# Mixers of a two-layer streaming trunk: four projected groups with the weights stationary and both token blocks moving, and one chain of small steps for both blocks

## The chip, the cores and the metric

The kernel runs on one core of a Trainium2 chip. The metric is device time in microseconds for one execution. Five engines work side by side, each on its own queue of instructions: TensorE (PE, matrix products and transposes into PSUM), VectorE (DVE), ScalarE (ACT), GpSimd (POOL) and SyncE (SP), which issues the DMAs here. Semaphores order them where one needs what another has made, or a buffer that another still reads.

## The reference

Two layers over 256 tokens of width 1024. Each layer is a half-step of a gated feed-forward network (1024 to 2 x 2816, back to 1024), then token mixers that read one combined input projection and are joined by one output projection, then a second feed-forward half-step. A residual with a factor and a layer norm close each of the three parts.

```python
for l in range(DEPTH):
    x = layer_norm(ALPHA * x + 0.5 * swiglu(x, ffn1_w_gu[l], ffn1_w_down[l]), ln1_g[l], ln1_b[l])
    h = x @ w_in[l]
    dq, dk, dv, mz, mxbc, mdt, gq, gk, gv, gz, gb, ga = jnp.split(h, IN_SPLITS, axis=-1)
    a_out = diff_attention_mixer(dq, dk, dv, ...)          # softmax maps, 4 heads
    m_out = mamba2_mixer(mz, mxbc, mdt, m_conv_w[l], ...)  # conv of 4 taps, silu, state-space, 8 heads
    g_out = gated_deltanet_mixer(gq, gk, gv, gz, gb, ga, g_conv_w[l], ...)  # conv, silu, triangular solve, 4 heads
    mix = jnp.concatenate([a_out, m_out, g_out], -1) @ w_out[l]
    x = layer_norm(ALPHA * x + mix, ln2_g[l], ln2_b[l])
    x = layer_norm(ALPHA * x + 0.5 * swiglu(x, ffn2_w_gu[l], ffn2_w_down[l]), ln3_g[l], ln3_b[l])
```

The depthwise convolution runs along the tokens, over mxbc (1024 channels) and over gq, gk and gv (768 channels). The solve in DeltaNet is against unit lower triangles of 64 x 64, one per head and chunk of 64 tokens.

## The kernel before

The 256 tokens are two blocks of 128. Weights come in units: by DMA into one of five raw buffers, then in two exact parts, the high part by a ScalarE cast (L230, wh) and the low part by a VectorE subtraction (L231, wl). A product is three: high by high, low by high, high by low (`mm3`, L219 to L226). The transposed tokens xh and xl are stationary, and 512 columns of weights move. Both blocks use a unit while it is there; block 1 follows block 0 by four units, five at the ends of a segment (`order`, L1019).

Each block has its own PSUM tiles: two of one bank for the large products (ps, po) and two for everything else (aux). The pools of small SBUF tiles are also per block.

A feed-forward group is a PSUM tile of 256 gate and 256 up columns. When it is complete, ScalarE takes the silu (sg, L395), VectorE multiplies (hh, L397), TensorE transposes hh twice (hTps) and the result is split into hT for the down projection.

In the mixers, the columns of w_in are projected in seven groups: qk (512 columns), v with the gates (272), dqk, m0, m1, mz and dvz (512 each). `job` spawns a chain of small steps behind each group and block. Groups that are convolved are copied out of PSUM by ScalarE token-major, transposed by TensorE (gqkps, gvps, mxps, mbcps: 56 transposes in the two layers), copied into xc with three columns of halo from the other block, and convolved: two taps on ScalarE, two on VectorE (L435 to L445), then silu. `after_qk` (L530) then makes squares (sq), their sums (ssps), a power on GpSimd (r), K·K and Q·K products (laps), and from these LA; ktok is a transpose of the keys. `inverse` (L671) solves the triangles in five doubling levels: products gps, G on VectorE (L698), products ups, a subtraction into TT (L715), a transpose T on VectorE (L693). `decays` (L465) makes the decay matrices: ar on GpSimd (L503), dps on TensorE, ex on ScalarE (L523). `after_dqk` does attention (scps, aps), `after_m0` and `after_m1` the state-space part (xsps, cbps, yps).

Chains are generators. A step yields a time, and its next step is emitted when that much TensorE work, times a factor from a table (`PACE`, one entry per step), has been emitted. The framework then orders instructions per engine and places the semaphores by tiles and buffers.

Of the kernel before, what the change touches and what calls it, by code (L numbers as in the profile page):

```python
# [27 lines left out]
TAPS = 2  # taps of the convolutions on ScalarE  # L28
SP = 2  # pieces in which a unit of weights is split
WS = 19  # tiles of half a bank for a block of tokens  # L30
# [5 lines left out]
PACE = {  # L36
    "after_v": (0.25, 1.49),
    "decays": (0.36, 0.48, 0.28, 1.01, 0.39, 0.56),
    "after_qk": (0.33, 0.24, 0.66, 0.33, 0.33, 0.33, 0.23, 0.33, 0.5, 0.2, 0.28, 0.33, 0.33, 0.28, 0.33),
    "after_m0": (0.33, 1.09, 0.78, 0.47, 0.78),  # L40
    "after_m1": (0.29, 0.19, 0.07, 0.14, 0.29, 0.24, 0.29),
    "after_mz": (0.39, 0.58, 0.58, 0.47, 0.58),
    "after_dqk": (0.41, 0.69, 0.27, 0.19, 0.27, 0.19, 0.54, 0.14, 0.41, 0.27),
    "after_dvz": (0.48, 0.71, 1.17, 0.39, 0.28, 1.12),
    "gdn_out": (0.12, 0.19, 0.23, 0.39),
    "norm": (0.28, 0.33),
    "after_gu": (4.67, 2.45, 2.33),
}
ORD = (1, 0, 4, 2, 3, 5, 6)
WORD = (4, 5, 2, 3, 6, 7, 0, 1)  # L50
# [3 lines left out]
# columns of the constants  # L54
# [6 lines left out]
# columns of w_in, in the order in which they are projected  # L61
WIN = (
    ("v", ((2824, 256), (3336, 8), (2304, 8))),
    ("qk", ((2312, 512),)),
    ("m0", ((1280, 512),)),
    ("m1", ((1792, 512),)),
    ("dqk", ((0, 512),)),
    ("mz", ((768, 512),)),
    ("dvz", ((512, 256), (3080, 256))),
# [7 lines left out]
def constants():  # L77
    """Masks, the identity and the rotary tables: they depend on shapes alone."""
# [21 lines left out]
class Kernel:  # L100
    def __init__(self, ctx, tc, a, out):
# [6 lines left out]
        self.w_p = [pool("wA", WS), pool("wB", WS)]  # L108
        self.h_p = [pool("hA", 5), pool("hB", 5)]
        self.s_p = [pool("sA", 20), pool("sB", 20)]  # L110
# [11 lines left out]
    def w(self, b, shape, name, dt=F32):  # L122
        assert int(np.prod(shape)) <= 528
        return self.w_p[b].tile([P, *shape], dt, tag="w", name=self.name(name))

    def h(self, b, shape, name, dt=F32):
        assert int(np.prod(shape)) <= 256
        return self.h_p[b].tile([P, *shape], dt, tag="h", name=self.name(name))

    def s(self, b, n, name):  # L130
        assert n <= 32
        t = self.s_p[b].tile([P, 32], F32, tag="s", name=self.name(name))
        return t[:, :n]

    def aux(self, b, name):
        return self.aux_p[b].tile([P, 512], F32, tag="aux", name=self.name(name))

# [1 line left out]
    def setup(self):  # L139
# [12 lines left out]
        self.neghalf = c.tile([P, 8], F32, name="neghalf")  # L152
# [7 lines left out]
    def setup_late(self):  # L160
        """What the mixers need, loaded and prepared behind the first products."""
# [53 lines left out]
    def mm3(self, ps, xh, xl, ws, start, stop):  # L215
        """ps[n] += x.T @ w[n] for the parts (xh, xl) and the list of (wh, wl)."""
# [50 lines left out]
    def ready(self, u, b):  # L267
        st = self.st[b]
        if u["kind"] in ("gu", "win"):
            return st["xseg"] == u["seg"] and len(st["xT"]) > u["part"] // 2  # L270
# [849 lines left out]
```

## Time and profile before

| | |
|---|---|
| runs (us) | 1134.03, 1136.46, 1136.87; median 1136.46 |
| profiled execution, span | 1134.7 us, its own time 1134.7 us from first to last instruction |
| TensorE busy | 1108.1 us, 5301 products and transposes |
| VectorE busy | 740.0 us, 1541 instructions |
| ScalarE busy | 590.4 us, 1250 instructions |
| DMA | 184.92 MB, mean 163 GB/s |
| mixers of layer 0 | about 202 to 345 us of the span |

A row of a group reads: line, engine, operation, output and inputs by name, shapes, count, then busy time and mean ns of one, then the idle time of the engine just before it and what ended that. A row of waits reads: engine and instruction, the releaser, then the sum in us, the times and the longest. A row of a window has start and end, its length, the busy time and count of PE, PEld, DVE, ACT and POOL, the granted TensorE clock as a part of full speed, the DMA share and GB/s. A row of the timeline has the start in us, the duration, and the instruction; x4 are four in a run. Durations of products overlap their neighbours, so the distance of starts tells what one takes.

### The profile page before, as it was taken

Reading aid. Unit: us, or ns where it says so; the run is one execution under the profiler, and the core shown is the slowest. Engines: PE = TensorE matmul, PEld = TensorE weight load, DVE = VectorE, ACT = ScalarE, POOL = GpSimd, SP = SyncE. Lnnn points to the kernel's source line nnn. Section 1 sums busy time; section 2 is a strip of 40 time slices with the busy share of each in tenths; the row PEclk is TensorE's granted clock in tenths of the full one; section 3 lists DMA queues with packets and bytes.
Section 4 is the critical chain, followed back from the end, with each engine's and each line's share of the span. In section 5 each row is a group of like instructions: output and inputs, shape, how many; then the busy total and the mean of one; then the engine's idle time right before and its main releaser. Section 6 shows DMA issues by size and latency. Waiting matters only on the chain.

```text
span 1134.7 us, 15487 instructions
## 1 busy us (share of the span) xinstructions
PE 1108.1 (98%) x5301; PEld 896.1 (79%) x5301; DVE 740.0 (65%) x1541; ACT 590.4 (52%) x1250; POOL 86.3 (8%) x123
## 2 busy tenths in 40 slices
PE   7999999999998999999999999999999999999996
PEld 6888888867887888888888888888688878888885
DVE  5565555896778955554575565477867887555545
ACT  5565444773674454554445454449546644555440
POOL 0000000032012100000000000001501120000001
PEclk9999999997999999999999999999989999999999
DMA  8775555631224565555575655555311347555650
GB/s 285 237 221 183 187 185 151 196 119 49 70 85 143 191 203 184 185 185 186 167 230 179 186 185 185 186 154 184 111 38 51 108 142 239 182 184 175 186 165 37
DMA packets 138374, 184.92 MB, mean 163 GB/s; under 512 B 15160, under 2 KB 111800, under 8 KB 138296
## 3 DMA queue, kind: packets, MB, share of 16 engines
q1 hardware_dynamic: 138296, 183.95, 52.2%
q8 instruction: 41, 0.67, 0.2%
q14 instruction: 37, 0.30, 0.1%
HBM read 182.86 MB, written 1.05 MB: 162 GB/s over the span
## 4 chain that ended last, share of the span: by engine, by line
PE 91%; DVE 5%; POOL 2%; ACT 1%; issue 1%; DMA 0%; SPq 0%; POOLq 0%; DVEq 0%; ACTq 0%
PE ps L219 18%; PE ps L220 18%; PE ps L226 16%; PE po L220 8%; PE po L219 8%; PE po L226 7%; PE ups L326 2%; PE ps L222 2%; PE gps L326 2%; PE hTps L235 2%; DVE wl L231 1%; PE scps L326 1%; PE xps L235 1%; POOL rsq L367 1%; PE yps L326 1%
## 5 line engine op out<-in xcount | busy, mean ns | idle before, releaser
L231 DVE TENSOR_TENSOR wl<-raw,wh 128x512 fp32r<-128x512 f32 (+1 forms) x672 | 437.5, 688 | 255.3 <-ACT wh L230 250.5
L230 ACT CAST wh<-raw 128x512 fp32r<-128x512 f32 (+1 forms) x672 | 380.8, 614 | 329.1 <-PE ps L226 186.6
L219 PE MATMUL ps<-wh,xh 128*128 128x512 f32 x928 | 374.8, 405 | 2.9 <-ACT wh L230 2.7
L220 PE MATMUL ps<-wl,xh 128*128 128x512 f32 x928 | 368.5, 397 | 0.0
L226 PE MATMUL ps<-wh,xl 128*128 128x512 f32 (+1 forms) x812 | 322.3, 398 | 0.0
L219 PEld LDWEIGHTS ps<-wh,xh 128*128 128x128 f32 x928 | 176.5, 190 | 39.4 <-ACT wh L230 3.3
L220 PEld LDWEIGHTS ps<-wl,xh 128*128 128x128 f32 x928 | 176.6, 190 | 37.3 <-DVE wl L231 1.8
L226 PEld LDWEIGHTS ps<-wh,xl 128*128 128x128 f32 x812 | 154.6, 190 | 35.0 <-issue 1.3
L219 PE MATMUL po<-wh,hT 128*128 128x512 f32 x352 | 139.1, 395 | 0.0
L220 PE MATMUL po<-wl,hT 128*128 128x512 f32 x352 | 138.2, 393 | 0.0
L226 PE MATMUL po<-wh,hT 128*128 128x512 f32 x336 | 105.6, 394 | 0.0
L220 PEld LDWEIGHTS po<-wl,hT 128*128 128x128 f32 x352 | 66.2, 188 | 14.7
L219 PEld LDWEIGHTS po<-wh,hT 128*128 128x128 f32 x352 | 66.1, 188 | 14.7
L226 PEld LDWEIGHTS po<-wh,hT 128*128 128x128 f32 x336 | 63.1, 188 | 14.0
L365 POOL TENSOR_SCALAR rs<-mv 128x1 f32<-128x1 f32 x12 | 6.5, 538 | 793.9 <-DVE mv L349 793.9
L397 DVE TENSOR_TENSOR hh<-ps,sg 128x256 f32<-128x256 f32 x88 | 37.0, 420 | 43.0 <-ACT sg L395 43.0
L395 ACT ACTIVATE sg<-ps 128x256 f32<-128x256 f32 x88 | 33.9, 385 | 55.0 <-PE ps L222 54.7
L222 PE MATMUL ps<-wh,xl 128*128 128x512 f32 (+1 forms) x116 | 46.0, 397 | 0.0
L230 ACT CAST hT<-hTps 128x256 fp32r<-128x256 f32 x88 | 32.5, 369 | 17.0 <-PE hTps L235 17.0
L231 DVE TENSOR_TENSOR hT<-hTps,hT 128x256 fp32r<-128x256 f32 x88 | 35.1, 420 | 0.1
L235 PE MATMUL hTps<-cst,hh 128*128 128x128 f32 x176 | 34.0, 272 | 0.0
L235 PEld LDWEIGHTS hTps<-cst,hh 128*128 128x128 f32 x176 | 24.6, 140 | 11.8
(247 smaller groups left out, 1008.3 us busy)
## 6 DMA issues: line engine op xcount, KB each, us to landing
raw<-in_ffn_w_gu_dram SPq DMA_DIRECT2D x352, 256.0 KB, 3.2
raw<-in_ffn_w_down_dram SPq DMA_DIRECT2D x88, 512.0 KB, 3.5
raw<-in_w_in_dram SPq DMA_DIRECT2D x40, 512.0 KB, 4.5
raw<-in_w_out_dram SPq DMA_DIRECT2D x16, 512.0 KB, 3.6
raw<-in_w_in_dram SPq DMA_DIRECT2D x24, 256.0 KB, 2.8
g<-in_ln_g_dram SPq DMA_DIRECT2D x6, 512.0 KB, 5.0
b<-in_ln_b_dram SPq DMA_DIRECT2D x6, 512.0 KB, 4.9
x<-in_x_dram SPq DMA_DIRECT2D x4, 256.0 KB, 5.8
```

Of the source, the lines that this page charges most:

```text
L219: mm(p, lhsT=xh, rhs=wh, start=start, stop=False)
L220: mm(p, lhsT=xh, rhs=wl, start=False, stop=False)
L222: mm(p, lhsT=xl, rhs=wh, start=False, stop=True)
L226: mm(p, lhsT=xl, rhs=wh, start=False, stop=False)
L230: self.nc.scalar.copy(hi, src)
L231: self.nc.vector.tensor_tensor(lo, src, hi.bitcast(F32), op=ALU.subtract)
L235: self.nc.tensor.transpose(ps[:, n * P : (n + 1) * P], t, self.ident)
L326: self.nc.tensor.matmul(out, lhsT=lhsT, rhs=rhs, start=start, stop=stop)
L365: nc.gpsimd.tensor_scalar(t, ap, mul, add, op0=ALU.mult, op1=ALU.add)
L367: nc.gpsimd.tensor_tensor(r, t, self.neghalf[:, :n], op=ALU.pow)
L395: nc.scalar.activation(sg, ps[:, 0:256], AF.Silu)
L397: nc.vector.tensor_mul(hh, ps[:, 256:512], sg)
```

## The change

Four groups of the input projection (qk, m0, v, m1) are projected the other way round: a 128 x 128 tile of weights is stationary and the transposed tokens of both blocks move, 256 columns at a time. PSUM then holds channels on partitions and the tokens of both blocks side by side, and the convolution reads it there. The token-major copies, the 56 transposes and the halo copies are gone. The other groups are dqk, gd (272: the attention's values and the gates), mz and gz, still per block. The order of groups is dqk, gd, qk, m0, v, m1, mz, gz.

The chains of decays, qk with the inverse, v, m0 and m1 run once, with both blocks' tokens (eight heads in the inverse). Attention stays per block. ar moves from GpSimd to VectorE. Products of laps, scps and rps that use different row groups of the array are emitted alternately.

PSUM is two tiles ps of two banks (both blocks, or both halves of an output) and four aux tiles of one bank. The SBUF pools are shared by the blocks. The table of paces is empty, so each step uses 0.39; a transpose counts 0.107 us rather than 0.213 in the emission clock, and `after_gu` yields 3. In feed-forward the blocks follow each other by one unit between the ends, five at the ends. Each product of the feed-forward is as before.

```diff
-NEAR = 4
-PACE = {
...
-}
-ORD = (1, 0, 4, 2, 3, 5, 6)
-WORD = (4, 5, 2, 3, 6, 7, 0, 1)
+PACE = {}
+WORD = (0, 1, 6, 7, 2, 3, 4, 5)
...
 WIN = (
+    ("dqk", ((0, 512),), None),
+    ("gd", ((512, 256), (3336, 8), (2304, 8)), None),
+    ("qk", ((2312, 512),), (256, 0, 384, 128)),
+    ("m0", ((1280, 512),), (0, 128, 256, 384)),
+    ("v", ((2824, 256),), (0, 128)),
+    ("m1", ((1792, 512),), (0, 128, 256, 384)),
+    ("mz", ((768, 512),), None),
+    ("gz", ((3080, 256),), None),
 )
...
-        self.ps_p = [pool("psA", 2, **psum), pool("psB", 2, **psum)]
-        self.aux_p = [pool("auxA", 2, **psum), pool("auxB", 2, **psum)]
+        self.ps_p = pool("ps", 2, **psum)
+        self.aux_p = pool("aux", 4, **psum)
...
+    def ps(self, name):
+        return self.ps_p.tile([P, 1024], F32, tag="ps", name=self.name("ps"))
...
+            if u["both"]:
+                for i, c0 in enumerate(u["tiles"]):
+                    o = g["ps"][:, 256 * i : 256 * i + 256]
+                    for kk in range(ks):
+                        k = u["part"] * ks + kk
+                        xh, xl = (t[:, :, k % 4, :] for t in self.xT[k // 4])
+                        s = slice(kk * width + c0, kk * width + c0 + P)
+                        end = last and kk == ks - 1
+                        for n, (a, x) in enumerate(((wh[:, s], xh), (wh[:, s], xl), (wl[:, s], xh))):
+                            self.nc.tensor.matmul(
+                                o, lhsT=a, rhs=x, start=k == 0 and n == 0 and i % 2 == 0, stop=end and n == 2,
+                                skip_group_check=True,
+                            )
...
-        ps = self.aux(b, name + "ps")
-        self.transposes([src[:, k * P : (k + 1) * P] for k in range(n)], ps)
-        xc = self.w(b, [n, P + 3], name + "xc")
-        nc.scalar.copy(xc[:, :, 3:], ps[:, : n * P].rearrange("p (k t) -> p k t", k=n))
...
+        x = ps[:, : 256 * n].rearrange("p (i t) -> p i t", i=n)
+        before = self.big([n, 256], name + "tap")
+        for j in range(0, n, 2):
+            pair = list(enumerate(tiles))[j : j + 2]
+            for i, t in pair:
...
+                    nc.scalar.activation(acc[:, i], x[:, i], AF.Copy, scale=col(3, t))
+                nc.scalar.activation(before[:, i, 1:], x[:, i, 0:255], AF.Copy, scale=col(2, t))
+            a = acc[:, j : j + 2, 1:]
+            nc.vector.tensor_add(a, a, before[:, j : j + 2, 1:])
+            for i, t in pair:
+                for k in (1, 0):
+                    d = 3 - k
+                    nc.vector.scalar_tensor_tensor(
+                        acc[:, i, d:], in0=x[:, i, 0 : 256 - d], scalar=col(k, t), in1=acc[:, i, d:],
+                        op0=ALU.mult, op1=ALU.add,
+                    )
...
+        for n in range(3):
+            ex = self.big([2, 4, P], "ex")
+            for b in range(2):
+                r = self.w([4, P], "ar")
+                ve.tensor_tensor(
...
-            for hd in range(4):
-                self.mm(pg[:, 64 * hd : 64 * hd + 64], lhsT=LT(hd), rhs=col1(T[:, hd, :], 0))
+            for e in range(8):
+                self.mm(pg[:, 64 * e : 64 * e + 64], lhsT=LT(e), rhs=col1(T[:, e, :], 0))
...
+        opening = lambda at, hi: max(1, LAG - at[1] // 2)
+        closing = lambda at, hi: min(LAG, max(1, LAG - (hi - at[0]) // 2))
+        phase(0, first, opening)
+        out.extend((None, i) for i in range(first, stop))
+        phase(stop, n, closing)
```

How this moves the instructions is seen at three places. Names carry a number for each tile.

The first is TensorE where m0's group (ps_2525) ends and v's (ps_2816) begins in layer 0. In the change the steps of qk follow seven products later:

```order
L288 MATMUL ps_2525<-xl_1871,wh_2324 128x256
L288 MATMUL ps_2525<-xh_1870,wl_2325 128x256
L288 MATMUL ps_2816<-xh_1847,wh_2415 128x256
L288 MATMUL ps_2816<-xl_1848,wh_2415 128x256
L288 MATMUL ps_2816<-xh_1847,wl_2416 128x256
...
L342 MATMUL ssps_2568<-cst,sq_2515 128x2 x8
L342 MATMUL laps_2589<-qk_2493 128x256
L342 MATMUL laps_2590<-qk_2493 128x256
```

On ScalarE, the convolution of qk (reading ps_2262, the tile that ps_2816 takes over) stands there among the exponentials of the decays (ex from dps) and weight casts:

```order
L558 ACTIVATE ex_2432<-dps_2441 128x512
L472 ACTIVATE qk_2493<-ps_2262,cw 128x256
L473 ACTIVATE gqktap_2494<-ps_2262,cw 128x255
L558 ACTIVATE ex_2432<-dps_2452 128x512
L472 ACTIVATE qk_2493<-ps_2262,cw 128x256
L473 ACTIVATE gqktap_2494<-ps_2262,cw 128x255
L226 CAST wh_2798<-raw_2467 128x512 x2
L472 ACTIVATE qk_2493<-ps_2262,cw 128x256
L473 ACTIVATE gqktap_2494<-ps_2262,cw 128x255
```

In the kernel before, no step of a convolution read ps; the tile was free after one copy.

The second place is the inverse on TensorE. Before, products of the groups (ps) and the other block's inverse stood between its levels:

```order
L326 MATMUL gps_2588<-T_2367,LA_2350 128x64
L326 MATMUL gps_2588<-T_2367,LA_2356 128x64
L219 MATMUL ps_2768<-wh_2307,xh_1987 128x512
L220 MATMUL ps_2768<-wl_2308,xh_1987 128x512
L226 MATMUL ps_2768<-wh_2307,xl_1988 128x512
L219 MATMUL ps_2768<-wh_2307,xh_1987 128x512
L326 MATMUL ups_2638<-TT_2366,G_2553 128x64 x4
```

Now eight heads go together, and the first three levels stand in a row behind v's last product, ahead of m1's group (ps_2972):

```order
L288 MATMUL ps_2816<-xh_1870,wl_2462 128x256
L342 MATMUL gps_2663<-T_2630,LA_2588 128x64 x4
L342 MATMUL gps_2663<-T_2630,LA_2605 128x64 x4
L342 MATMUL ups_2679<-TT_2629,G_2634 128x64 x8
L342 MATMUL gps_2706<-T_2630,LA_2588 128x64 x4
L342 MATMUL gps_2706<-T_2630,LA_2605 128x64 x4
L342 MATMUL ups_2722<-TT_2629,G_2689 128x64 x8
L342 MATMUL gps_2741<-T_2630,LA_2588 128x64 x4
L342 MATMUL gps_2741<-T_2630,LA_2605 128x64 x4
L288 MATMUL ps_2972<-xh_1847,wh_2517 128x256
```

VectorE has m0's convolution (xsT from ps_2525) between the steps of these levels:

```order
L751 TENSOR_TENSOR G_2634<-gps_2663,cst 128x256x2
L475 TENSOR_TENSOR xsT_2776<-xsT_2776,mxtap_2777 128x2x255
L479 SCALAR_TENSOR_TENSOR xsT_2776<-ps_2525,cw,xsT_2776 128x254
L768 TENSOR_TENSOR TT_2629<-TT_2629,ups_2679 128x256x2
L479 SCALAR_TENSOR_TENSOR xsT_2776<-ps_2525,cw,xsT_2776 128x253
L746 STREAM_TRANSPOSE T_2630<-TT_2629 128x1024
L479 SCALAR_TENSOR_TENSOR xsT_2776<-ps_2525,cw,xsT_2776 128x254
L479 SCALAR_TENSOR_TENSOR xsT_2776<-ps_2525,cw,xsT_2776 128x253
L751 TENSOR_TENSOR G_2689<-gps_2706,cst 128x128x4
```

The third place is the end of a feed-forward group on TensorE. Block 0's last product is L218 here; five products of the next group (ps_1010) follow, and then block 1's last six in the same tile ps_906:

```order
L218 MATMUL ps_906<-wh_820,xl_156 128x512
L215 MATMUL ps_1010<-wh_841,xh_130 128x512
L216 MATMUL ps_1010<-wl_842,xh_130 128x512
L222 MATMUL ps_1010<-wh_841,xl_131 128x512
L215 MATMUL ps_1010<-wh_841,xh_130 128x512
L216 MATMUL ps_1010<-wl_842,xh_130 128x512
L215 MATMUL ps_906<-wh_820,xh_155 128x512
```

Before, block 1 had a tile of its own, some twenty products behind.

More of the change, by code (lines that the diff above doesn't have):

```diff
@@ L267, in ready @@
     def ready(self, u, b):
-        st = self.st[b]
         if u["kind"] in ("gu", "win"):
-            return st["xseg"] == u["seg"] and len(st["xT"]) > u["part"] // 2
-        return u["k"] // 2 in st["hT" if u["kind"] == "down" else "mT"]
+            n = u["part"] * u["ks"] // 4
+            return all((u["seg"], n, i) in self.xready for i in ((0, 1) if u["both"] else (b,)))
+        return (u["k"] // 2, b) in (self.hT if u["kind"] == "down" else self.mT)
     def job(self, u, b):
-        st = self.st[b]
@@ new lines, in job @@
+            last = u["part"] == KD // ks - 1
+            if u["both"]:
[11 more added lines that the diff above has]
+                            )
+                        self.clock += 3 * 256 / 2400
+                    if i < len(u["tiles"]) - 1:
+                        self.step()
+                if last:
+                    self.spawn(u["then"](u, g["ps"]))
+                return
@@ L647, in after_qk @@
[L647 to L659 removed]
+            LA.append(t)
@@ new lines, in after_qk @@
+            yield 0.5
+        b4 = lambda t: t.unsqueeze(2).to_broadcast([P, 4, 64])
+        x4 = self.h(0, [4, 64], "x4")
+        de = self.s(0, 4, "de")
+        ve.tensor_mul(de, d[:, 0:4], erev[:, 0, 0:4])
+        pk = self.aux(0, "ktok")
+        self.transposes([qk[:, 0, 0:P], qk[:, 2, 0:P]], pk)
+        ve.tensor_tensor(x4, pk[:, 0:256].rearrange("p (h d) -> p h d", h=4), b4(de), op=ALU.mult)
+        TT = yield from self.inverse(LA)
+        yield from self.until("gv")
+        rhs = self.w([8, 64], "rhs")
@@ L728, in inverse @@
-        yield 0.9
-        return TT
-    def after_m0(self, l, b, ps):
-        nc, st = self.nc, self.st[b]
-        hm = self.w(b, [512], "hm")
-        nc.scalar.copy(hm, ps)
-        yield 0.8
-        xsT = self.conv(l, b, hm, (0, 1, 2, 3), "m", "mx")
-        yield 6
-        yield from self.until(b, "E")
-        pt = self.aux(b, "xsps")
-        self.transposes([xsT[:, k] for k in range(4)], pt)
+            ve.tensor_tensor(cols(TT, 1), cols(TT, 1), view(pu), op=ALU.subtract)
+        yield 1.5
@@ L792, in after_m1, with after_mz @@
-        if b == 1:
-            yield 0.2
-            pf = self.aux(b, "yfps")
+        ve.tensor_add(y[:, 1], y[:, 1], t)
+        self.mx["y"] = y
+    def after_mz(self, l, b, ps):
+        nc = self.nc
+        ve = nc.vector
+        if b == 0:
+            self.sz = self.big([2, 512], "sz")
+        sz = self.sz
+        nc.scalar.activation(sz[:, b], ps, AF.Silu)
+        if b == 0:
+            return
+        yield 0.3
+        yield from self.until("y")
+        y = self.mx["y"].rearrange("p b h d -> p b (h d)")
+        ss = self.s(b, 4, "mss")
+        for i in range(2):
+            ve.tensor_mul(y[:, i], y[:, i], sz[:, i])
@@ L808, in after_m1 @@
[L808 to L824 removed]
+                q = self.h(b, [256], "msq")
@@ L996, in mix @@
             units = []
-            for name, cols in (WIN[i] for i in ORD):
-                for part in range(4):
+            for name, cols, tiles in WIN:
+                group = {}
+                width = sum(n for _, n in cols)
+                ks = 4 if width == 256 else 2
+                for part in range(KD // ks):
                     units.append(
-                        dict(kind="win", l=l, w=a["w_in"][l], name=name, part=part, cols=cols,
-                             width=sum(n for _, n in cols), then=self.after_win)
+                        dict(kind="win", l=l, w=a["w_in"][l], name=name, part=part, cols=cols, width=width, ks=ks,
+                             group=group, both=tiles is not None, tiles=tiles, then=self.after_win)
                     )
```

904 lines of the change are left out of this document (437 added, 467 removed).

## The prediction

> **What bounds the kernel now.** I read the page first, then the waits of TensorE, then the clock.
>
> ```profile
> span 1134.7 us, 15487 instructions
> PE 1108.1 (98%) x5301; PEld 896.1 (79%) x5301; DVE 740.0 (65%) x1541; ACT 590.4 (52%) x1250; POOL 86.3 (8%) x123
> PE xps L235 <- DMA x<-in_x_dram: 4.2, 1, 4.2
> PE ktok L235 <- DVE LA L576: 4.0, 2, 2.0
> PE mTps L235 <- DVE y L827: 3.2, 4, 1.1
> PE ps L219 <- ACT wh L230: 2.7, 1, 2.7
> PE dops L326 <- DVE mT L231: 2.1, 2, 1.1
> PE dps L326 <- POOL ar L503: 0.6, 2, 0.3
> PE mTps L235 <- DVE do L954: 0.5, 2, 0.3
> PE laps L326 <- DVE ss L550: 0.4, 2, 0.2
> 345.00:800.00 455.00, 452.78 (x2081) 367.11 (x2081) 292.63 (x557) 232.57 (x478) 20.34 (x29) 1.00 0.59 183
> ```
>
> TensorE is busy 1108.1 of 1134.7 us. Its waits sum to 17.7 us: 6.9 at the start (xps, wh), the other 10.8 in the mixers, 5.4 a layer, none longer than 2.0. In the long stretch of feed-forward (the row 345 to 800; its columns run PE, PEld, DVE, ACT, POOL, then clock) TensorE is busy 452.8 of 455 us at full clock. So nothing is to be won there, and the mixers hold what can be won or lost besides TensorE's own work. The third thing is the clock:
>
> ```profile
> 250.00:300.00 50.00, 50.00 (x269) 39.90 (x268) 34.94 (x91) 24.23 (x61) 11.89 (x15) 0.86 0.22 64
> 260.00:262.00 2.00, 2.00 (x17) 1.88 (x17) 0.88 (x4) 0.36 (x1) 1.16 (x1) 1.00 0.82 249
> 264.00:268.00 4.00, 4.00 (x13) 2.95 (x13) 2.83 (x11) 0.00 (x0) 0.36 (x1) 0.50 0.00 0
> 800.00:820.00 20.00, 17.79 (x88) 13.02 (x86) 15.94 (x42) 9.07 (x21) 9.12 (x8) 0.91 0.42 119
> 820.00:834.00 14.00, 14.00 (x54) 10.58 (x53) 8.48 (x26) 3.45 (x14) 3.04 (x5) 0.63 0.07 19
> ```
>
> The granted clock falls to 0.50 once in each layer's mixers. It costs 50 x 0.14 = 7.0 us in layer 0 and 20 x 0.09 + 14 x 0.37 = 7.0 us in layer 1. From 260 to 262 TensorE was busy all the time, though only with small float32 products, and the clock fell right after.
>
> **TensorE's work, -3 us a layer.** Prices are distances from start to start, since products overlap:
>
> ```profile
> 202.02 0.40 PE L220 MATMUL ps<-wl,xh 128*128 128x512 f32 x1
> 205.27 0.39 PE L219 MATMUL ps<-wh,xh 128*128 128x512 f32 x1
> 207.34 0.29 PE L219 MATMUL ps<-wh,xh 128*128 128x272 f32 x1
> 207.98 0.29 PE L226 MATMUL ps<-wh,xl 128*128 128x272 f32 x1
> 208.10 0.68 PE L235 MATMUL gqkps<-cst,hq 128*128 128x128 f32 x4
> 208.54 0.37 PE L219 MATMUL ps<-wh,xh 128*128 128x272 f32 x1
> 208.75 0.29 PE L220 MATMUL ps<-wl,xh 128*128 128x272 f32 x1
> ```
>
> Fourteen products of 512 columns lie between 202.02 and 205.27: 0.232 us each. Five of 272 columns take 207.34 to 207.98: 0.128. The line through both gives an estimate of 0.121 for 256 columns, which the trace has not in this form. Four transposes take 208.10 to 208.54, 0.11 each, and the product behind them comes 0.21 rather than 0.128 later, 0.08 for the way back. A layer gives up 192 products of 512 columns (44.5 us) for 384 of 256 (46.5): +2.0. The 28 transposes of the token-major projections go: -3.1, and some 14 returns from them: -1.1. The cumulative sums and C·B products change shape, about -0.5. Sum: -2.7, say -3. The copies out of PSUM, halo copies and half of the short DVE steps that vanish were beside TensorE and give nothing by themselves.
>
> The laps, scps and rps products now alternate between row groups of the array. Side by side they could take half: laps 1.05 us for four and scps 0.64 for four here,
>
> ```profile
> 243.58 1.13 PE L326 MATMUL laps<-gqkacc 64*128 64x256 f32 x4 [0.19 <-DVE ss L550]
> 255.02 0.71 PE L326 MATMUL scps<-dkT,dqT 32*128 32x128 f32 x4
> 308.30 0.45 PE L326 MATMUL sps<-vnew,x 128*64 128x64 f32 x8
> ```
>
> that is 4.2 us a layer for sixteen laps, 2.6 for sixteen narrow scps and 4.2 for sixteen wide ones, at the price of a laps. The halves give at most -5.5. That such pairs can overlap is shown by sps, which alternate between column halves: the row behind those eight starts at 308.68, 0.048 each. What follows is VectorE work on each result, though, so most of it would turn into waiting. I take -1, bounds 0 and -5.5.
>
> By the Trainium skill, TensorEngine Tiling (Array Packing), Key Properties, different tiles of the array load and multiply in parallel; by that alone the sum would be about 9 us lower for both layers. The sps row agrees for column halves, and no row of before has row groups alternating.
>
> **The waits of the mixers, +15 us a layer.** Four groups now leave one PSUM tile for both blocks, and there are two such tiles. The convolution reads PSUM directly, so the group after next cannot begin until its last step is done. All prices of that chain:
>
> ```profile
> L693 DVE STREAM_TRANSPOSE T<-TT 128x512 f32<-128x512 f32 x20 | 14.0, 698 | 0.0
> L445 DVE SCALAR_TENSOR_TENSOR gqkacc<-gqkxc,cw,gqkacc 128x128 f32<-128x128 f32 x32 | 8.7, 345 | 0.0
> L698 DVE TENSOR_TENSOR G<-gps,cst 128x256 f32<-128x256 f32 x20 | 8.4, 422 | 16.9 <-PE gps L326 15.6 <-POOL ar L503 0.9 <-POOL G L691 0.3
> L576 DVE SCALAR_TENSOR_TENSOR LA<-laps,d,ex 128x256 f32<-128x256 f32 x16 | 6.8, 458 | 1.1 <-PE laps L326 0.8
> L231 DVE TENSOR_TENSOR wl<-raw,wh 128x512 fp32r<-128x512 f32 x656 | 431.2, 694 | 255.3 <-ACT wh L230 250.5 <-DMA raw<-in_ffn_w_gu_dram 0.6
> L437 ACT ACTIVATE gqkacc<-gqkxc,cw 128x128 f32<-128x128 f32 x16 | 6.3, 392 | 0.2
> L523 ACT ACTIVATE ex<-dps 128x512 f32<-128x512 f32 x12 | 7.2, 598 | 4.0 <-PE dps L326 3.8
> L552 POOL TENSOR_TENSOR r<-ss,neghalf 128x8 f32<-128x8 f32 x4 | 8.4, 2112 | 12.2 <-DVE ss L550 12.2
> 252.70 1.00 PE L326 MATMUL gps<-T,LA 128*128 128x64 f32 x8
> 253.54 0.56 PE L326 MATMUL csps<-a,cst 128*128 128x12 f32 x4
> ```
>
> Twice as wide, by these rows, a conv step is 0.46 us on VectorE (the LA row) and about 0.47 on ScalarE, an addition or mask of 512 columns 0.69 (the wl row), and TT's 1024 columns 1.2. gps of eight heads are sixteen of 0.105, 1.7 us.
>
> First, v. ScalarE's order puts the first conv steps of qk among the last exponentials of the decays, so from the last dps on there run: an exponential 0.6, two ScalarE steps 0.9, a pair of channel tiles on VectorE 0.69 + 4 x 0.46 = 2.5, then ScalarE's four steps of the second pair 1.9 (its copies share a tile with the first pair), and that pair on VectorE 2.5: 8.4 us. TensorE has 22 products of m0 left, 2.6. Wait for PSUM before v: **5.8**. Behind it in TensorE's queue stand ssps, laps and ktok, so all of DeltaNet is late by it.
>
> Second, the squares. Silu and square of 1024 columns, about 2.3 behind the conv, against seven products, 0.8: **1.5**. Then the power on POOL (2.1, its row), small steps and two LA (0.9) against 4.2 us of laps: **0.7**, between nothing and the 2.0 that ktok waits in a layer of before, and nearer the 2.0 should the laps run in pairs.
>
> Third, the first gps. Six LA 2.75, x4 0.4, two masks and the identity 2.6, two weight splits 1.4, the transpose 1.2: 8.3 us against ktok and 41 products of v, 5.1: **3.2**.
>
> Fourth, the levels. Before, one block's inverse had the other block's and full products between its steps; now eight heads go together and the first levels stand in a row. For each, TensorE waits 0.7 for G, then 0.7 (subtraction) + 0.46 (a conv step of m0 queued ahead on VectorE) + 1.2 (transpose): 3.0 twice, **6.0**. From the third level on m1's products lie between.
>
> Together 17.2. The mTps, dops and dps waits (3.2 a layer of the 5.4) I leave as they are, so +17.2 - 2.2 = +15. Bounds: start-to-start on VectorE and ScalarE is shorter than duration, and an earlier conv could halve the first wait, so from below +4; from above +22, if half clock stretches the chain.
>
> **The clock, +2.5 us a layer.** A wait of 5.8 us in one piece and then 20 us of small products with gaps replace a stretch that cost 7.0 already. At half clock ssps, laps and two levels (2 + 4 + 7 us at full clock) would cost 13 more if none of it were hidden; The 41 products of v between them are dense work, at which the clock stood at 1.00 (the row 345 to 800). I take 9.5 in place of 7.0; bounds -5 and +8.
>
> By the Trainium skill, TensorE: Matmul & The Clock Gate, Part 1, the clock halves after an idle window of about 3.4 us and comes back after a busy one; by the idle wait alone it would cost, as an estimate, near 2 us a layer, and the sum would be some 15 us lower. The rows from 260 on differ: there the clock fell with TensorE busy, so small products count as little activity, and I go by them.
>
> **Feed-forward, 0.** One PSUM tile holds both blocks, so block 1's last six products wait for block 0's VectorE product.
>
> ```profile
> 108.79 0.40 PE L222 MATMUL ps<-wh,xl 128*128 128x512 f32 x1
> 109.23 0.39 ACT L395 ACTIVATE sg<-ps 128x256 f32<-128x256 f32 x1 [1.04 <-PE ps L222]
> 109.64 0.42 DVE L397 TENSOR_TENSOR hh<-ps,sg 128x256 f32<-128x256 f32 x1 [1.00 <-ACT sg L395]
> ```
>
> From the start of block 0's last product to the end of hh is 1.27 us; that product and the five between are 6 x 0.232 = 1.39. It is covered by 0.1 us. If hh finds VectorE in a weight split (0.69), each of 88 such places can lose 0.1 or so: bounds 0 and +9.
>
> **Sum.** Per layer -3 - 1 + 15 + 2.5 = +13.5, for two +27: 1134.7 + 27 = 1161.7 for a profiled execution. The median of the runs, 1136.46, stands 1.8 above it, so **1163.5 us**, +2.4%. What a measurement of this kernel can tell from no change is about 0.3%, 3.4 us.
>
> **Rivals.**
> Covered (0.14): the conv ends before m0's products do, the levels find products between, and waits and clock stay as they were. Then the work decides: 1136.5 - 6 = 1130, down to 1121 with all pairs. For it: VectorE is busy 65%, ScalarE 52%, and both lose work. Against: with two PSUM tiles TensorE has nothing else it may begin. It decides where the conv ends within 2.6 us of the last dps, against 8.4.
> Level (0.08): the chain's waits come out near 4 a layer above before's, which the work repays: 1133 to 1140.
> Clock (0.12): half clock from v's wait to the third level, all of it on the chain: 15 us more a layer would be the most, 8 is likelier, 1163.5 + 2 x 5.5 + FFN's 9 = 1184.
> Weight load (0.03): a load is busy 190 ns,
>
> ```profile
> L219 PEld LDWEIGHTS ps<-wh,xh 128*128 128x128 f32 x928 | 176.5, 190 | 39.4 <-ACT wh L230 3.3
> ```
>
> and a 256-column product as short as 0.121 might wait for them: 768 x 0.07 = +54, 1217. Against it: the 272-column products follow each other every 0.128 with such loads.
>
> **How the numbers follow.** The forecast itself has 0.63, and 1145 to 1180 as its own range. The range of 8 in 10 reaches down into the level case, since those bounds are wide, and up into the clock case: 1138 to 1188. Faster by over 0.3%: 0.14; within: 0.08; slower: 0.78.
>
> **What would show it.** Among TensorE's waits: one on the conv's scalar_tensor_tensor of qk (4 to 7 us in each layer), on T and TT (2 to 4 each, several), hardly any in feed-forward; 256-column products every 0.12; half clock between 250 and 300. I am wrong if the wait before v is under 2 us, if 256-column products take over 0.14, or if feed-forward shows waits of tenths in most groups.

## The result, and the profile after

The changed kernel takes 1181.84 us (median of 4 runs, 1180.58 to 1183.86), the kernel before beside it 1135.51: a ratio of 1.0411, 95% interval 1.0395 to 1.0428. It is slower by 46 us where the prediction had 27, inside the predicted range of 1138 to 1188. The profiled execution has a span of 1182.0 us, 47.3 above before's 1134.7. Ratios are taken over the runs within 1.5% of the fastest of their kernel; only the first kernel with late steps, further down, has others, four of its ten.

The head of the changed kernel's page:

```profile
span 1182.0 us, 15784 instructions
PE 1111.2 (94%) x5613; PEld 920.3 (78%) x5613; DVE 721.0 (61%) x1371; ACT 541.7 (46%) x1126; POOL 55.0 (5%) x65
```

VectorE, ScalarE and GpSimd all have less to do than before (ScalarE 541.7 us for 590.4, GpSimd 55.0 for 86.3), while TensorE's busy time hardly moves. Its share of the span falls from 98% to 94%. The waits of TensorE in the changed kernel (sum in us over both layers, times, longest):

```profile
PE ps L288 <- DVE qk L479: 13.3, 2, 6.6
PE gps L342 <- DVE T L746: 12.5, 6, 2.4
PE ktok L231 <- DVE LA L624: 8.6, 2, 4.3
PE mTps L231 <- DVE do L989: 4.3, 2, 2.1
PE ups L342 <- DVE G L751: 3.4, 4, 0.9
PE aps L231 <- DVE sm L951: 3.2, 2, 1.6
PE yps L342 <- DVE ex L830: 2.7, 2, 1.4
PE mTps L231 <- DVE y L882: 1.5, 2, 0.8
PE mTps L231 <- ACT dv L493: 1.4, 2, 0.7
PE mTps L231 <- DVE go L712: 1.3, 2, 0.6
PE ps L215 <- DVE hh L425: 0.4, 1, 0.4
```

The mixers' waits are some 26 us a layer where they were 5.4: before v (qk), before the products of the inverse (T and G), before ktok (LA), and several shorter ones in attention and at the end. Feed-forward has one wait of 0.4.

The last step of block 1's normalisation tells where a segment ends. These two rows of VectorE's timeline are the start and the end of layer 0's mixers in the changed kernel:

```profile
207.96 0.21 DVE L365 BATCH_NORM_AGGREGATE mv<-stats 128x2 f32<-128x12 f32 x1
410.26 0.20 DVE L365 BATCH_NORM_AGGREGATE mv<-stats 128x2 f32<-128x12 f32 x1
```

And these are the same two in the kernel before:

```profile
206.58 0.20 DVE L349 BATCH_NORM_AGGREGATE mv<-stats 128x2 f32<-128x12 f32 x1
385.15 0.20 DVE L349 BATCH_NORM_AGGREGATE mv<-stats 128x2 f32<-128x12 f32 x1
```

The mixers take 202.3 us in place of 178.6, so 23.7 more a layer, and 47.4 for two is all of the loss. The clock of the changed kernel, in stretches of the span (columns as before: length, then PE, PEld, DVE, ACT and POOL, then the granted clock):

```profile
250.00:275.00 25.00, 16.24 (x87) 12.03 (x85) 13.93 (x28) 14.62 (x28) 4.24 (x4) 0.83 0.26 76
275.00:300.00 25.00, 18.41 (x102) 16.78 (x102) 15.16 (x27) 3.94 (x9) 7.42 (x6) 0.64 0.13 42
300.00:325.00 25.00, 19.31 (x89) 18.81 (x89) 10.45 (x16) 2.89 (x6) 0.00 (x0) 0.50 0.00 1
400.00:500.00 100.00, 99.87 (x455) 79.29 (x454) 65.48 (x118) 51.10 (x106) 2.41 (x3) 1.00 0.66 200
```

An account of a layer's mixers follows from such windows 2 us long, added up between those rows of both layers and halved: idle time of TensorE is length less busy, and what the clock costs while it works is busy time x (1 - clock). The third column is what is left of the 23.7. The same account is used for the experiments below; it is that of the one profiled run of each kernel.

| us a layer, against before | idle | clock | work at full clock |
|---|---|---|---|
| predicted | +15 | +2.5 | -4 |
| changed kernel | 26.5 - 5.5 = +21.0 | 20.4 - 6.8 = +13.6 | -10.9 |

So the change does give TensorE less work, nearly three times what I forecast, and pays for it three times over in idle time and clock. The forecast total came nearer than its parts: idle time and clock were 17 us a layer too low, and the work that I had missed took 7 of them back.

### The profile page after: what moved, and what is told of

It reads as the page before. It is cut to its first block, busy times and chain, and to the rows that moved or that the text cites. A ratio compares the mean times of both kernels' runs of the same rounds, so it can differ in the third digit from the quotient of the medians.

```text
span 1182.0 us, 15784 instructions
## 1 busy us (share of the span) xinstructions
PE 1111.2 (94%) x5613; PEld 920.3 (78%) x5613; DVE 721.0 (61%) x1371; ACT 541.7 (46%) x1126; POOL 55.0 (5%) x65
## 4 chain that ended last, share of the span: by engine, by line
PE 81%; DVE 9%; DMA 3%; ACT 3%; issue 2%; POOL 2%; SPq 1%; POOLq 0%; DVEq 0%; ACTq 0%
PE ps L215 15%; PE ps L216 14%; PE ps L222 13%; PE po L215 6%; PE po L216 6%; PE po L222 6%; PE ps L288 6%; PE ups L342 3%; DVE wl L227 3%; PE gps L342 2%; PE ps L218 2%; PE hTps L231 2%; DMA raw<-in_ffn_w_gu_dram 1%; PE dps L342 1%; ACT wh L226 1%
## 5 line engine op out<-in xcount | busy, mean ns | idle before, releaser
L215 PE MATMUL ps<-wh,xh 128*128 128x512 f32 (+2 forms) x832 | 329.2, 397 | 4.0 <-ACT wh L226 3.3
L216 PE MATMUL ps<-wl,xh 128*128 128x512 f32 (+2 forms) x832 | 320.2, 385 | 0.0
L222 PE MATMUL ps<-wh,xl 128*128 128x512 f32 (+2 forms) x728 | 283.4, 389 | 0.7
L215 PEld LDWEIGHTS ps<-wh,xh 128*128 128x128 f32 x832 | 157.0, 189 | 45.5 <-DVE hh L425 13.2
L288 PE MATMUL ps<-xh,wh 128*128 128x256 f32 x224 | 69.3, 310 | 13.3 <-DVE qk L479 13.3
L288 PE MATMUL ps<-xl,wh 128*128 128x256 f32 x224 | 69.5, 310 | 0.0
L288 PE MATMUL ps<-xh,wl 128*128 128x256 f32 x224 | 68.5, 306 | 0.0
L288 PEld LDWEIGHTS ps<-xh,wh 128*128 128x128 f32 x224 | 47.2, 211 | 14.1 <-ACT qk L484 13.6
L288 PEld LDWEIGHTS ps<-xl,wh 128*128 128x128 f32 x224 | 47.4, 212 | 1.3 <-issue 1.1
L288 PEld LDWEIGHTS ps<-xh,wl 128*128 128x128 f32 x224 | 47.1, 210 | 1.0 <-issue 1.0
```

The lines of the kernel that those rows point to most:

```text
L215: mm(p, lhsT=xh, rhs=wh, start=start, stop=False)
L216: mm(p, lhsT=xh, rhs=wl, start=False, stop=False)
L222: mm(p, lhsT=xl, rhs=wh, start=False, stop=False)
L288: self.nc.tensor.matmul(o, lhsT=a, rhs=x, start=k == 0 and n == 0 and i % 2 == 0, stop=end and n == 2, skip_group_check=True,)
```

## The experiments

Each is timed against the kernel before on the same chip; the changed kernel stood at 1.0411 of before.

**The GpSimd fills.** After the power on GpSimd, VectorE's smallest steps take as long as the fills of G that follow the power. The timeline of the changed kernel there, all engines in order of time (start, length, engine, line, operation, tiles; in brackets the idle time before it and what ended it):

```profile
281.78 3.62 POOL L744 MEMSET G<- 128x1024 f32 x4
281.95 0.16 DVE L607 TENSOR_TENSOR nk<-r,ss 128x8 f32<-128x8 f32 x1
282.03 3.40 DVE L608 TENSOR_SCALAR rq<-r 128x8 f32<-128x8 f32 x1
285.64 3.22 DVE L624 SCALAR_TENSOR_TENSOR LA<-laps,d,ex 128x256 f32<-128x256 f32 x8
286.65 0.66 PE L231 MATMUL ktok<-cst,qk 128*128 128x128 f32 x2 [4.30 <-DVE LA L624]
```

GpSimd fills from 281.78 on, four times 0.9 us. The step on VectorE that makes rq from r has eight elements in a partition and takes 3.40 us; LA follows it, and ktok on TensorE waits 4.30 for LA. The experiment fills G on ScalarE:

```diff
-            nc.gpsimd.memset(G, 0.0)
+            nc.scalar.activation(G, self.ident.unsqueeze(1).to_broadcast([P, G.shape[1], P]), AF.Copy, scale=0.0)
```

> The changed kernel, but the five zero fills of G in the inverse are made by ScalarE (a copy of the identity with scale 0) and no longer by GpSimd. Theory, GpSimd in the way: in the changed kernel VectorE's small step rq takes 3.40 us in both layers, exactly while GpSimd runs four fills (3.62 us); without them it takes about 0.2, TensorE's wait for ktok falls from 4.3 to about 1 us a layer, and the time falls by 2 x 3.4 and a little for the clock, from 1182 to 1172 to 1176 us. Rival, the power sets it: rq only stands in the row by chance and laps at half clock come last anyway; the wait stays over 3 us and the time is within 3 us of 1182.

Measured: 1178.53 us, ratio 1.0373 [1.0349, 1.0397]. The same step in the timeline of this kernel:

```profile
281.06 0.17 DVE L608 TENSOR_SCALAR rq<-r 128x8 f32<-128x8 f32 x1
```

And two of its waits of TensorE:

```profile
PE ktok L231 <- DVE LA L624: 2.2, 2, 1.1
PE ps L215 <- DVE bc L479: 5.1, 2, 2.6
```

The mechanism is as the theory had it, 3.40 against 0.17 us, and ktok's wait falls by 3.2 a layer. The time falls by only 3.3 in all: idle time, 26.5 in the changed kernel, is 24.8 in one layer and 26.5 in the other, because mz's first product now waits 2.6 us for the conv of m1, the tile it takes over. The place was right, the price half of what was expected. By the Trainium skill, SBUF — State Buffer, section Who interferes with whom, VectorE in a two-port mode, which tensor_scalar can enter, and GpSimd lock each other out for whole instructions. The rows fit that, as rq is a tensor_scalar and starts 0.25 us behind the first fill; here it was held through four fills in a row. That rq ran in such a mode is not shown.

**The tile that the convolution holds.** One copy on ScalarE, of 1024 columns, empties the PSUM tile, and the conv reads the copy:

```diff
-        x = ps[:, : 256 * n].rearrange("p (i t) -> p i t", i=n)
+        x = self.big([n, 256], name + "cp")
+        nc.scalar.copy(x, ps[:, : 256 * n].rearrange("p (i t) -> p i t", i=n))
```

> The changed kernel, but each convolution first copies its PSUM tile to SBUF in one ScalarE step (1024 columns, about 1.1 us) and reads the copy, so the tile is free for the group after next. Theory, the held tile: the 6.6 us wait before v goes, v's 48 products run before the squares, and m1's products stand between the first levels of the inverse, where TensorE waits 8 us for T and G; waits fall from 26 to about 12 us a layer and the clock stays up longer: 1150 to 1160 us. Rival, the chain of qk: it is one us longer by the copy, sets the end, and products moved ahead are missing later (first gps, mTps): 1175 to 1185 us.

Measured: 1158.24 us, 1.0196 [1.0163, 1.0229], half of the loss back. Three waits of TensorE in this kernel:

```profile
PE gps L342 <- DVE T L747: 15.9, 4, 6.0
PE ktok L231 <- DVE LA L625: 4.8, 2, 2.5
PE ssps L342 <- ACT sq L586: 3.9, 2, 2.0
```

The wait before v is gone; the levels of the inverse have m1's products between them (TensorE waits for T twice a layer, not three times, and for G not at all). Part of it comes back in front of the first gps, 6.0 us, since v's products now run earlier: idle time is 19.5 a layer, and the clock costs 13 to 18 in place of 20.4. Both theories had a share, the held tile the larger.

**Eight heads in one chain.** The inverse as two chains of four heads, one per block:

```diff
             LA.append(t)
+            self.spawn(self.inverse(t, b))
...
-        TT = yield from self.inverse(LA)
+        yield from self.until(("TT", 0), ("TT", 1))
```

> The changed kernel, but the inverse runs as two chains of four heads, one per block, as before the change; everything else is still merged. Theory, eight heads in one chain: while one block waits for T or G, the other's products run; TensorE's waits for T, G and TT fall from 8 to about 3 us a layer, its time falls by 2 x 4 to 2 x 7, to 1168 to 1174 us. Rival: VectorE's steps are twice as many and set the pace, the waits only change their names: within 3 us of 1182.

Measured: 1187.30 us, 1.0456 [1.0423, 1.0489], slower than the changed kernel and than both ranges. TensorE's waits for T and G fall from 8.0 to 5.7 us a layer, not to 3, and mz's first product now waits 4.1 for the conv of m1. Idle time does fall, to 24.1 a layer, but the clock costs 23.6 and 25.9: TensorE is fed by the other block's small products, and the clock stays down. In this order, with nothing larger to put between the levels, taking the heads apart wins nothing; whether merging them costs time in another order is not shown.

**The clock by itself.** Added products of 512 columns that nothing reads, where TensorE would wait:

```diff
+    def warm(self, n):
+        pw = self.aux(0, "warm")
+        xh = self.xT[0][0]
+        for _ in range(n):
+            self.nc.tensor.matmul(pw, lhsT=xh[:, 0, 0, :], rhs=xh[:, 0], start=True, stop=True)
...
         self.conv(l, ps, qk, (2, 0, 3, 1), "g", "gqk")
+        self.warm(26)
...
             ve.transpose(out=flat(T), in_=flat(TT))
+            if n in (1, 2):
+                self.warm(8)
```

> The changed kernel with added products that nothing reads: 26 of 512 columns (6.0 us) ahead of m0's last products, where TensorE would wait for the conv of qk, and 8 (1.9 us) behind ups of each of the first two levels, where it would wait 2.4 us for T. They fill waits and do no useful work; they are there to keep the granted clock up. Theory, the clock is a cost of its own: squares, laps and levels run at full clock (squares 1.8 rather than 3.6 us, gps and ups of a level 1.8 each rather than 3.65), the waits of these places are filled, and the time falls by 2 x 6 to 2 x 10 us, to 1162 to 1170 us. Rival, the half clock lies under VectorE's chain: the added work costs as much as it wins, 1178 to 1188 us.

Measured: 1170.49 us, 1.0297 [1.0263, 1.0331]: 42 useless products per layer make the kernel 11 us faster. The squares, the laps, ups of the first level and gps of the second in the changed kernel, from TensorE's timeline:

```profile
275.07 3.58 PE L342 MATMUL ssps<-cst,sq 128*128 128x2 f32 x16
278.57 3.78 PE L342 MATMUL laps<-qk 64*128 64x256 f32 x16
297.88 3.67 PE L342 MATMUL ups<-TT,G 128*128 128x64 f32 x16 [0.85 <-DVE G L751]
303.97 3.65 PE L342 MATMUL gps<-T,LA 128*128 128x64 f32 x16 [2.42 <-DVE T L746]
```

The same in this kernel, with ktok:

```profile
274.78 1.95 PE L342 MATMUL ssps<-cst,sq 128*128 128x2 f32 x16
276.66 2.00 PE L342 MATMUL laps<-qk 64*128 64x256 f32 x16
284.74 0.66 PE L231 MATMUL ktok<-cst,qk 128*128 128x128 f32 x2 [6.08 <-DVE LA L631]
294.94 3.02 PE L342 MATMUL ups<-TT,G 128*128 128x64 f32 x16 [0.85 <-DVE G L760]
301.28 2.49 PE L342 MATMUL gps<-T,LA 128*128 128x64 f32 x16
```

Squares take 1.95 us where they took 3.58, and the second level's gps 2.49 where they took 3.65; the first level's gps take 1.97 in both kernels. The laps are faster too, 2.00 for 3.78, but nothing is won there: from the first of them to ktok it is 8.08 us in both kernels, because ktok waits 6.08 for LA where it waited 4.30. At that place the rival holds.

The clock costs 13.8 and 12.2 us a layer rather than 20.4. Idle time is 9.1 lower and the work, with the added products, 10.6 higher, which nearly cancel, and a layer's mixers are 5.9 shorter. So most of the clock's cost that was taken away here had been a cost of its own and not hidden under VectorE's chain. The filling is not perfect (the clock still falls while TensorE waits 6.1 us for ktok), so this is a lower bound. By the Trainium skill, TensorE: Matmul & The Clock Gate, Part 1, an idle window of some 3.4 us halves the clock and a busy one restores it. In the changed kernel the 6.6 us wait does that: it ends at 273.35, and the clock is 1.00 from 266 to 268 and 0.50 from 270. In the levels no wait is over 2.4 us, and the clock stands at 0.50 from 300 to 325 with TensorE busy 19.31 of 25 us, up to 317.97 with small products alone.

**Row groups.** laps, scps and rps in their old order:

```diff
-            for j in range(2):
-                for p in range(2):
+            for p in range(2):
+                for j in range(2):
```

(and so for scps and rps)

> The changed kernel with the products of laps, scps and rps in their old order, so that neighbours use the same row group of the array. Theory, the pairs are a gain of TensorE's own: the wide scps of the changed kernel take 0.13 us each rather than 0.26, so scps cost 3.4 us a layer more, laps about 2 at full clock, 4 at half: 1187 to 1193 us. Rival, as the prediction priced it: laps lie under the wait for LA (8.0 us from the first laps to ktok) and attention's steps wait for VectorE anyway: 1182 to 1185 us.

Measured: 1187.03 us, 1.0446 [1.0427, 1.0466]. The number falls in the first theory's range, but the run doesn't show what it says: eight wide scps still take 1.06 us, read in TensorE's timeline from their start to the start of the next product:

```profile
227.04 1.14 PE L342 MATMUL scps<-dkT,dqT 32*128 32x256 f32 x8
228.10 0.39 PE L215 MATMUL ps<-wh,xh 128*128 128x272 f32 x1
```

In the kernel before, four of them take as much, 1.06:

```profile
293.32 1.13 PE L326 MATMUL scps<-dkT,dqT 32*128 32x256 f32 x4
294.38 0.66 PE L326 MATMUL ups<-TT,G 128*128 128x64 f32 x4
```

So two row groups run side by side whether single products alternate or pairs of them, as long as both stand next to each other in the queue. The rps, which now come four and four, lose some of it: 1.54 us for sixteen rather than 1.04. The 5 us therefore came mostly from elsewhere. In the profiled run a layer's mixers are 1.4 us longer: idle time is 1.6 higher, with the same new wait of mz for the conv of m1 (2.6 us) as with the fills on ScalarE, the work is 1.4 higher, and the clock costs 1.6 less. The overlap as TensorE's work is read from the rows: 1.06 saved on each eight wide scps, 0.65 on each eight narrow ones, 3.4 us a layer. What it is worth in time, this run doesn't show.

The same part alone in the kernel before:

```diff
-            pl = self.aux(b, "laps")
+        pls = [self.aux(b, "laps") for _ in range(2)]
...
+            if i % 2 == 0:
+                pis = [self.aux(b, "scps") for _ in range(2)]
```

> The kernel before with one part of the change alone: laps and scps alternate between row groups. TensorE is the bound there, so if the overlap is a real gain the time falls by up to 2 x 5.4 us, to 1125 to 1131 us. Rival, aux tiles taken in pairs make the block's next steps wait (there are two to a block), or the steps behind wait for VectorE: 1133 to 1140 us.

Measured: 1144.41 us, 1.0062 [1.0039, 1.0086], slower than before and than both ranges. laps and scps overlap there too, and a layer's work at full clock is 1.9 lower, but idle time rises from 5.5 to 9.0 a layer and the clock's cost from 6.8 to about 10; mTps waits more for y and do. TensorE was the bound, and still less work for it did not come out as time.

**Order.** First the copy and the fills on ScalarE together, the edits of the first two experiments:

> The changed kernel with both the copy of each convolution's PSUM tile and the zero fills on ScalarE. Theory, the two causes are separate places: the copy gave 23.6 us, the fills 3.3, together 1154 to 1156 us. Rival, with the tile free the fills no longer hold anything (rq takes 0.73 us there rather than 3.40): 1157 to 1160 us.

Measured: 1159.49 us, 1.0198 [1.0174, 1.0223]: the fills add nothing once the tile is free. On top of both, the steps of the qk chain are put later. The number behind a `yield`, times the pace of 0.39, is how much of TensorE's work, in us of the emission clock, comes before the chain's next step; WORD is the order of the parts of w_out. The ones changed are those behind the squares, behind LA of block 1, in a level before gps and before ups, and behind the last step of o:

```diff
-WORD = (0, 1, 6, 7, 2, 3, 4, 5)
+WORD = (0, 1, 2, 3, 4, 5, 6, 7)
...
-        yield 7
+        yield 22
...
-            yield 0.5
+            yield 0.5 if b == 0 else 7
...
-            yield 4 if n == 0 else 1.5
+            yield 12 if n == 0 else 4.5
...
-            yield 1.5
+            yield 2.0
...
-        yield 4
+        yield 20
```

> As the kernel with copy and zero fills, and the steps of the qk chain emitted later (22, 7, 12, 4.5 and 2 in place of 7, 0.5, 4, 1.5 and 1.5; attention's last step 20 in place of 4; the output projection takes DeltaNet's part last), so that products of m1 and mz stand where TensorE waits for squares, LA and T. Theory, the waits of the chain are a matter of order once PSUM is free: waits for sq, LA and T fall from 12 to under 5 us a layer, half clock with them, 1135 to 1145 us. Rival, the chain is too long for the mixers: late steps run out of products at the end, new waits on vnps, rps and mTps take their place, 1150 to 1165 us.

Measured: 1138.21 us as the median of ten runs that lie between 1125.3 and 1151.7, wider than any other kernel's; the ratio is 0.9989 [0.9960, 1.0017]. The spread goes with TensorE's mean granted clock, which is on record for each run: 0.987 at 1125.3, 0.973 to 0.979 in the five runs from 1134.2 to 1138.8, and 0.960 to 0.963 in the four from 1148.7 to 1151.7. The profiled run is the fastest of the ten, and even there the layers differ: the clock was 0.94 in the stretch of layer 0's mixers (200 to 400) and 1.00 in layer 1's (775 to 975), with idle time of 11.7 and 12.6. What decides whether the clock falls is not shown. Three more sets follow, with waits that were left moved as well. The second, against this one:

```diff
-            yield 0.5 if b == 0 else 7
+            yield 0.5 if b == 0 else 13
...
-        yield 0.6
+        yield 6
...
-            yield 12 if n == 0 else 4.5
+            yield 9 if n == 0 else 4
...
-        yield 4
+        yield 9
...
-        yield 20
+        yield 34
```

> The kernel with late steps, with four waits aimed at that its trace still had: 57 products instead of none between laps and ktok (waited 3.6 us a layer), attention's last step later (34 in place of 20; mTps waited 2.1), its transposes later (9 in place of 4; aps waited 1.6 and 1.0), DeltaNet's last transposes later (6 in place of 0.6; waited 2.1). Theory, each wait is a place in the order: 1118 to 1130 us, and with fewer gaps fewer falls of the clock, so the runs lie closer together than 1125 to 1152. Rival, the chain's length decides now and 57 are too many: the end of the mixers waits, 1135 to 1150 us.

Measured: 1131.95 us, 0.9966 [0.9946, 0.9986], a little faster than before and just outside both ranges; its ten runs are 1127.0 to 1139.5. The third, against the second, gives the inverse shorter steps from its second level on and LA of block 1 less room:

```diff
-        yield 22
+        yield 20
...
-            yield 0.5 if b == 0 else 13
+            yield 0.5 if b == 0 else 10
...
-            yield 9 if n == 0 else 4
+            yield 10 if n == 0 else 3.5
...
-            yield 2.0
+            yield 1.8
```

> As the one beside it, but ktok directly behind laps (its wait of 3.6 us stays) and shorter steps in the levels (3.5 and 1.8 in place of 4 and 2), so that the chain ends earlier and has more products left at its end. Theory, the chain's length decides: as fast or faster than the one beside it, 1118 to 1130 us. Rival, the wait for ktok costs its 3.6 us a layer and the clock behind it: 1130 to 1145 us, slower than the one beside it.

Measured: 1152.40 us, 1.0144 [1.0115, 1.0172]. Shorter steps and the wait for ktok cost more than they save; the rival held, and more than it. Idle time hardly differs from the second set's (12.8 us a layer against 12.3 in the profiled runs, of which the second set's is its fastest); what differs is the clock, which costs 19.8 a layer against 4.9. The wait of 3.6 us for ktok, which the second set had filled, is there again, as it is in the first set; that the clock falls because of it fits, but isn't shown. The fourth is the second with later steps of the decays and behind the conv of m:

```diff
-        yield 4
+        yield 7
...
         self.conv(l, ps, xsT, (0, 1, 2, 3), "m", "mx")
...
-        yield 7
+        yield 14
```

> The kernel with copy, zero fills and the second set of late steps, with two more places moved: m0's transposes later (14 in place of 7; xsps waited up to 2.6 us) and the cumulative sums later (7 in place of 4; csps waited 1.1). That also puts 25 products of v between laps and ktok rather than 57 of m1. Theory, waits are places in the order: waits fall by 3 to 5 us a layer, 1122 to 1130 us, below the kernel before. Rival, the steps behind these (decays, yps) come too late in their turn: 1130 to 1140 us.

Measured: 1128.25 us, 0.9926 [0.9913, 0.9939], five runs within 1126.6 and 1129.6: 8 us faster than the kernel before. But the waits didn't fall as the theory had it: idle time is 11.8 us a layer against 12.3, and m0's transposes (xsps) still wait up to 2.9. The fastest runs of both sets agree (1126.6 and 1127.0); the median is lower because the runs lie closer together, at a granted clock of 0.984 to 0.988 rather than 0.977 to 0.988. The head of its page:

```profile
span 1124.8 us, 15781 instructions
PE 1083.2 (96%) x5613; PEld 895.3 (80%) x5613; DVE 710.5 (63%) x1371; ACT 558.2 (50%) x1144; POOL 45.4 (4%) x55
```

Its layer 0, mixers and the stretches beside them, as one window:

```profile
200.00:400.00 200.00, 187.93 (x1234) 163.80 (x1233) 152.68 (x323) 108.25 (x236) 17.99 (x19) 0.97 0.43 130
```

And its laps, from TensorE's timeline:

```profile
268.16 2.00 PE L342 MATMUL laps<-qk 64*128 64x256 f32 x16
270.09 0.39 PE L288 MATMUL ps<-xh,wl 128*128 128x256 f32 x1
```

Idle time is 11.8 a layer, the clock costs 5.8, and the work at full clock is 9.7 below before's: +6.3, -1.1 and -9.7 make, rounded, -4.4 a layer; the ratio gives -4.2. At full clock sixteen laps take 1.93 us, where before's price makes 4.2. Last, the second set without the copy:

> The same late steps and zero fills as in the second set, but without the copy: the convolutions read PSUM as in the change. Theory, the held tile is a cause by itself: the wait of 5 to 7 us a layer before v stays, whatever the order of the small steps, and the clock falls behind it: 1145 to 1160 us. Rival, order is all there is and the copy's gain was only that it moved v ahead of the squares: 1130 to 1140 us.

Measured: 1154.72 us, 1.0154 [1.0133, 1.0174]. Two of its waits of TensorE:

```profile
PE ps L288 <- DVE qk L479: 9.6, 2, 4.8
PE ps L288 <- DVE xsT L479: 4.0, 2, 2.1
```

With the late order the held tile still costs 4.8 us before v and 2.1 before m1. The second set differs in the copy alone and is 22.8 us faster by the medians, 21 by the ratios: the copy is worth about as much in a good order as in the first (23.6). In the profiled runs the held tile costs 7.4 us a layer in idle time (19.7 for 12.3) and 7.0 in the clock (11.8 for 4.9).

## Why the prediction was right in its direction and short in its size

- **What bounds it.** Right: feed-forward had nothing to give, and all 47 us are in the mixers. The cover of 0.1 us was enough: in the 88 places there is one wait of 0.4.
- **TensorE's work, -3.** The price of a 256-column product was 0.121 by the line through two rows; in the changed kernel's timeline the second row below starts seven products after the first, 0.84 us later, 0.12 each. The rival of the weight load is refuted by that. Both terms of work together were -4, and the account above has -10.9.

```profile
231.82 0.28 PE L288 MATMUL ps<-xh,wl 128*128 128x256 f32 x1
232.66 0.28 PE L288 MATMUL ps<-xh,wh 128*128 128x256 f32 x1
```

- **Pairs, -1.** As TensorE's work this was mis-sized: I took the low end of a bound of 5.5, on the argument that the saving would turn into waiting, and left rps unpriced. scps save 3.4 us a layer, laps 2.2 at full clock and rps 1.0. Those 6.6 with the 2.7 of the term above make 9.3 of the 10.9; 1.6 stay unnamed. What the pairs are worth in time is not shown: the run with the old order kept most of the overlap, and in the kernel before the saved work did come back as waiting and half clock, as the argument had it.
- **Waits, +15.** Measured +21.0. The chain before v was read rightly: 6.6 for 5.8, with one weight split of 0.68 us among VectorE's conv steps that I had not counted; T and G together are 8.0 for 9.2, and the squares waited 0.2 for 1.5. Two steps failed. ktok, 0.7 in the sum, was 4.3: the power took 2.90 us where I had 2.1, and I never put the four fills queued behind it on GpSimd, which I had in the listing, beside VectorE's small steps. And the 3.2 a layer that I left as they were became 4.2 (do 2.1, y 0.8, dv 0.7, go 0.6), with 1.6 for aps and 1.4 for yps beside them, in attention and at the end, which no term covered.
- **The clock, +2.5.** The step that failed most: +13.6, beyond its upper bound of 8. I counted ssps, laps and two levels at half clock and let v's dense products restore it. They did, but late: the clock was at 0.50 from 270 on, some sixteen of v's 41 products ran at half before it came back at 290, and near 297 it fell again, to stay at 0.50 until near 328, through the second and third level, the first one's ups and the start of m1's products. That makes about 55 us of half clock a layer in place of 13.7. Part of it looks like a circle: at half clock a level's gps take 3.65 us rather than 1.89 (the latter in the fourth set with late steps), VectorE gets their result later, and the stretch without dense products grows. No run takes this circle apart from the waits by itself; the added products show only that most of what they took off the clock's cost came out as time.
- **The rivals.** The covered case did not come about in this kernel. The late orders with the copy come out at 1128 us, near the 1130 worked out for it, but by other terms: 9.7 less work a layer rather than 3, and 6.3 more waiting rather than none. The argument against it, that with two PSUM tiles TensorE has nothing else to begin, is what the copy and its removal show. The order of the groups, ar on VectorE and the shared pools were not tried by themselves.

## What to carry to other kernels

A PSUM tile that is read by a long chain of small steps holds up the group after next; one copy that frees it early was worth 23 us here, though it makes the chain itself longer. When a chain is merged and loses what stood between its steps, price the clock with the waits: idle time and small products together kept TensorE at half speed for four times as long. And of every engine that a chain passes, look at what is queued right behind its step: four fills on GpSimd held VectorE's 0.17 us step for 3.40, although freeing it won only 3.3 us in all, since another wait took its place.

## What the runs showed of the hardware

- Products in two row groups of the array overlap in full: eight wide scps take 1.06 us, as long as four of one group, also when they come two and two. Sixteen rps (64 columns, 64 rows) take 1.04 us in the changed kernel, as long as eight of one group in the kernel before, 1.03, both at full clock. From the timeline of before:

```profile
321.37 1.10 PE L326 MATMUL rps<-S,gqkacc 64*128 64x64 f32 x8
322.40 0.50 PE L226 MATMUL ps<-wh,xl 128*128 128x512 f32 x1
```

And from that of the changed kernel:

```profile
352.89 1.11 PE L342 MATMUL rps<-S,qk 64*128 64x64 f32 x16
353.93 0.50 PE L216 MATMUL ps<-wl,xh 128*128 128x512 f32 x1
```

- Useless dense products in TensorE's waits can make a kernel faster (1170.5 against 1181.8 us).
- Idle time alone does not tell whether the clock falls: in the first kernel with late steps the two layers of one execution had 11.7 and 12.6 us of idle time, and the clock cost 11.9 us in the first and nothing in the second.
